# Final state products of three head groups made in the hole of the second norm of a decoder step

## The chip, the core and the metric

The kernel runs on one core of one Trainium2 chip and is written against the engines directly: TensorE (PE, with its weight loads PEld shown apart), VectorE (DVE), ScalarE (ACT), GpSimd (POOL) and SyncE (SP), which issues most DMAs. The metric is the device time of one execution in microseconds, as the median of repeated runs.

## The reference, cut to what matters

The reference is one step of a one-layer hybrid decoder: 256 prompt tokens (two chunks of 128) and 64 sample tokens (8 sequences of 8) with a width of 2048, all in fp32.

```python
h = rms_norm(x, norm_mix_pre); proj = h @ w_in        # gMLP u, v | SSD z, x, B, C, dt
gate_out = gelu(u) * (tril(W_s) @ layer_norm(gelu(v)) + b_s)       # chunks of 128
ssm_out, new_ssm = ssd_mixer(z, xbc, dt, state, ...)               # 32 heads of 64, 4 groups
x = x + rms_norm(concat(gate_out, ssm_out) @ w_out, norm_mix_post) # the second norm
f = (gelu(g) * u) @ ffn_w_down,  g, u = split(conv(rms_norm(x, norm_ffn_pre) @ ffn_w_up))
x = x + rms_norm(f, norm_ffn_post)
```

Inside the SSD mixer the state of a head runs over the two prompt chunks. The state after the last chunk is an output of its own (`ssm_state_prompt`, `o_ssm_p` in the kernel): the state after chunk 0, decayed by the whole of chunk 1, plus the sum over the tokens s of chunk 1 of (decay from s to the end) * dt_s x_s B_s^T. This sum is the "final state product" below. For a group of 8 heads it is one product of a 128x128 matrix (tokens by state) with a 128x512 matrix (tokens by 8 heads of 64), in plain fp32. Nothing else in the step needs it.

## The kernel before, in words

All 320 tokens lie in the free dimension of one tile per 128 features (`NT` = 320, `KD` = 16 tiles for the width of 2048). Every large product is taken as three: weights and activations are split into a high part rounded to fp32r and a low part, the remainder, and `ps` gathers hi x hi, lo x hi and hi x lo (L153, L154, L155; L190 for the first block of the up projection, whose products go through all column blocks with the high part of the weights first). The weights come through SP in slabs of 512 KB (`wraw`, three buffers). For each slab ACT writes the high part (`whi`, L124) and DVE subtracts it for the low part (`wlo`, L125), each in one instruction of 128x1024. `split` (L401, L402) does the same for activations: ACT scales and rounds, DVE makes the remainder.

The stages follow one another on PE: projection and gMLP part; four SSD head groups, whose steps are written as generators (`ssd(g)`) and pulled along by the projections that run around them (`tick`), so that their small products lie scattered between the weight products; `w_out` in eight chunks of features (`chunk_out`), summed into `acc`; the second norm; `ffn_w_up` and `ffn_w_down`; the last norm.

A tile framework orders the instructions of each engine by their place in the program, by priorities (`first()` and `high_priority` pull work ahead), and by `issue_after(x)`, which keeps an instruction behind x. It also puts in the waits between engines. PSUM has two pools of four banks each: `mm` for the weight products and `misc` for the small ones (tags `mm` and `ms`). Each `misc` call takes the next bank and waits until that bank's last reader is done.

At the end of `ssd(g)` the kernel makes `x1d`, the decayed inputs of chunk 1 (L851, POOL, a tile named `xde`), and decays the state of chunk 0 in place (`s1`, L1027, POOL). The generator `final()` then makes the final state product into `fin_ps` (L1032, PE), adds it to `s1` (L1034, DVE) and stores it. Groups 0 to 2 do this inside the group. Group 3's is kept in the list `rest` for the second norm.

The second norm is the one place where PE has no large products ready. Behind the last product of `w_out` come the token sums of squares (`tsum`, L294), group 3's final state product, and the root: DVE scales (L279, L281), ACT takes the square root (L282), DVE refines the inverse root (L283 to L286). PE spreads the result over the partitions with three transposes (`spread`, L302). Meanwhile `idle_products` (L817) has PE make products that nobody reads: one of 128x512 ahead of the spread, seven behind it, all fp32r. Then `x1_ready(k0, nk)` makes the blocks of the normed input one by one, each through DVE scale (L1141), DVE add of the residual (L1142), ACT high part (L401) and DVE low part (L402). The first products of `ffn_w_up` (L190) take each block as soon as it is there. POOL has little to do in that stretch; it makes squares for norms (L335) in others. On SP, behind the last weight slabs of the groups, come `cs` loads (L837, from `dacs_d`), the small loads of the last group's norm (L324), and then the slabs of `w_out`.

Of the kernel before, what the change touches and what calls it, by code (L numbers as in the profile page):

```python
# [9 lines left out]
F32 = mybir.dt.float32  # L10
F32R = mybir.dt.float32r
I32 = mybir.dt.int32
AF = mybir.ActivationFunctionType
ALU = mybir.AluOpType
# [3 lines left out]
P = 128  # L18
# [3 lines left out]
NT = NP + NS  # L22
# [12 lines left out]
def hybrid_step(  # L35
# [10 lines left out]
    act, dve, pool, pe, sp = nc.scalar, nc.vector, nc.gpsimd, nc.tensor, nc.sync  # L46
# [4 lines left out]
    dr = ctx.enter_context(tc.tile_pool(name="dr", bufs=1, space=DRAM))  # L51
# [5 lines left out]
    def misc(name):  # L57
        return ms.tile([P, 512], F32, tag="ms", name=name)
# [6 lines left out]
    with tc.high_priority(offset=300000):  # L65
        dve.memset(ones, 1.0)

        ps = misc("early")
# [31 lines left out]
    def col(i):  # L100
        return prm[:, i:i + 1]
# [166 lines left out]
        rsqrt_ins.append(ins)  # L268
        return r

    rsqrt_ins, sums_ins, spread_ins, rooted, low = [], [], [], [], []

    def rsqrt_by_root(rest, ps, scale, rows=P):

# [14 lines left out]
    def token_sums(*sqs):  # L289

        ps = misc("tsum")
        for c, o in enumerate((0, P, NT - P)):
            for i, sq in enumerate(sqs):
                ins = pe.matmul(ps[:, c:c + 1], sq[:, o:o + P], ones[:, 0:1], start=i == 0, stop=i == len(sqs) - 1).ins  # L294
        sums_ins.append(ins)
        return ps[:, 0:3]
# [40 lines left out]
    def squares_of(total):  # L337

        one, held = [], []

        def step(nb):
            if nb < KD - 3:
                add_square(total, acc[:, nb, :], nb == 0)
                if nb == 0:

                    act.activation(tp.tile([P, 1], F32, name="root_there", bufs=1), total[:, 0:1], AF.Sqrt)
                return
            with first():
                if nb < KD - 1:
                    held.append(misc("sq_ps")[:, :NT])  # L350
                else:
                    one.append(tp.tile([P, NT], F32, tag="sq", name="sq", bufs=2))
                for ts in parts_of(nb):
                    act.activation((one or held)[-1][:, ts], acc[:, nb, ts], AF.Square)
                if nb > KD - 3:
                    dve.tensor_tensor(out=total, in0=total, in1=held.pop(0), op=ALU.add)
        return step, one


    dacs_d = dr.tile([NH, NT + NS], F32, name="dacs_d")  # L360
    tot_d = dr.tile([NH, NB], F32, name="tot_d")
    ssq_d = [dr.tile([P, NT // 32], F32, name=f"ssq_d{i}") for i in range(4)]


# [30 lines left out]
    def split(hi, lo, x, scale=None):  # L395

        if scale is None:
            act.copy(hi, x)
            made = dve.tensor_tensor(out=lo, in0=x, in1=hi.bitcast(F32), op=ALU.subtract)
        else:  # L400
            act.activation(hi, x, AF.Copy, scale=scale)  # L401
            made = dve.scalar_tensor_tensor(out=lo, in0=x, scalar=scale, in1=hi.bitcast(F32), op0=ALU.mult, op1=ALU.subtract)  # L402

        return made.ins
# [16 lines left out]
    with ExitStack() as mctx:  # L421
        op = mctx.enter_context(tc.tile_pool(name="op", bufs=1))
# [153 lines left out]
        with tc.tile_pool(name="gp", bufs=1) as gp:  # L576
# [60 lines left out]
            for n in range(2):  # L637
                ps = banks("ps_v")
                for kt in range(KD):
                    x = [h[:, kt, :] for h in hT], xs_two[kt // 8][:, kt % 8, :]  # L640
                    cs = V0 + 1024 * n
# [38 lines left out]
                with first():  # L680
                    for c, g in ((0, 0), (0, 1), (1, 0), (1, 1), (2, 0), (2, 1)):
                        at, src = slice(0, NS if c == 2 else P), ps[c][g]
                        if c == 2:
# [4 lines left out]
                                                       scale=r[at, c:c + 1]).ins)  # L688
# [99 lines left out]
        with tc.tile_pool(name="sd", bufs=1) as sd:  # L788
# [23 lines left out]
            x_of = {0: x0}  # L812
            rest = []

            def idle_products(ps, n):
                for _ in range(n):
                    ins = pe.matmul(ps, bsp[:, 0, :P], bsp[:, 0, :], start=True, stop=True).ins  # L817
                return ins

            def ssd(g):  # L820

                xs = x_of[g]
# [125 lines left out]
                def end(i, by=act):  # L948
                    made = grown(sts[i], bms.pop(i))
                    store_state(i, sts[i], by)  # L950
                    return made
# [75 lines left out]
                pool.tensor_tensor(out=by_head(s1), in0=by_head(s1),  # L1027
                                   in1=dec[:, 2, h0:h0 + 8].unsqueeze(2).to_broadcast([P, 8, 64]), op=ALU.mult)

                def final():  # L1030
                    ps = misc("fin_ps")
                    made = pe.matmul(ps, btok[:, 1, bs], x1d, start=True, stop=True)  # L1032
                    yield made.ins
                    dve.tensor_tensor(out=s1, in0=s1, in1=ps, op=ALU.add)  # L1034
                    (pool if g == 3 else act).dma_start(o_ssm_p[g], s1)
                    yield
                if g == 3:
                    rest.extend([lambda: end(3, pool), final()])
                else:
                    yield  # L1040
                    yield
                    for _ in final():
                        pass

            tasks = [ssd(g) for g in range(4)]
            res = [[] for _ in range(4)]
# [50 lines left out]
            finish(norm3)  # L1097
            sq2 = hp.tile([P, NT], F32, tag="ssq", name="sq2")

            squares, one = squares_of(sq2)  # L1100
            chunk_out(w_out, 7, *res[3], False, squares, apart=True)

# [4 lines left out]
            with first():  # L1107
                with tc.issue_after(pd_last[-1]), tc.issue_after(added_last[0]):
                    made = rest[0]()
                with tc.issue_after(made):  # L1110
                    most = token_sums(sq2)
                with tc.issue_after(sums_ins[-1]):
                    ps = token_sums(*one)
                with tc.issue_after(sums_ins[-1]):
                    made = next(rest[1])
                r = rsqrt_by_root(most, ps, 1.0 / D)
                behind = rsqrt_ins[-1]

                idle = misc("idle")
                with tc.issue_after(made):  # L1120
                    made = idle_products(idle, 1)
                with tc.issue_after(made):
                    r2b = spread(r)
                with tc.issue_after(spread_ins[-1]):
                    idle_products(idle, 7)
            sq3 = hp.tile([P, NT], F32, tag="ssq", name="sq3")


# [6 lines left out]
            def x1_ready(k0, nk):  # L1135
                for kt in range(k0, k0 + nk):
                    q, k = kt // 4, kt % 4
                    a = acc[:, kt, :]
                    with first() if kt < 2 else tc.high_priority(offset=100000):
                        with tc.issue_after(added[0]) if kt == 1 else nullcontext():  # L1140
                            dve.scalar_tensor_tensor(out=a, in0=a, scalar=col(prm_at["norm"][0] + kt), in1=r2b, op0=ALU.mult, op1=ALU.mult)  # L1141
                        added.append(dve.tensor_tensor(out=a, in0=a, in1=xr[q][:, k, :], op=ALU.add).ins)  # L1142
                        low.append(split(hT[0][:, kt, :], hT[1][:, kt, :], a, col(prm_at["norm"][1] + kt)))
                        if k == 3 and q < 2:
                            load_x(q + 2)
            load_x(0)
            load_x(1)
            up0 = []
            project(ffn_w_up, 0, None, late=up0, ready=x1_ready, after=behind, ahead=1, more=DFF, held=added)
            with tc.issue_after(low[2]):  # L1150
                next(rest[1])

            room = [op.tile([P, 4, NT], F32, tag="xs", name="sq_two", bufs=2) for _ in range(2)]
            total, *some = [t[:, i:i + 2, :] for t in room for i in (0, 2)]
# [7 lines left out]
    x1 = acc  # L1162
# [273 lines left out]
```

## Time and profile before

| what | value |
|---|---|
| time, median of 3 runs | 1775.49 us (1774.15 to 1775.97) |
| the profiled execution's own time | 1774.69 us |
| span in its profile | 1773.0 us |
| PE busy | 1765.1 us, 100% |
| PE weight loads | 1711.9 us, 97% |
| DVE busy | 1173.7 us, 66% |
| ACT busy | 817.9 us, 46% |
| POOL busy | 274.5 us, 15% |
| granted TensorE clock | 0.999 of full |
| moved by DMA | 290.01 MB |

The span runs from the first to the last instruction that the profiler saw; the execution's own time has a little more around it. Busy times are sums over the whole span, so they tell which engine is the bound on average and not in which stage. A row of the timeline reads: start in us, duration in us, engine, source line, operation, written tile <- read tiles, shape, and the number of like instructions that follow one another in it; the brackets give the idle time before it and who ended it. A row of a group reads: smallest / median / largest duration in ns, then the first and the last start.

### The profile page before, as it was taken

The numbers are of one execution on the slowest core, as the hardware profiler recorded it, in microseconds if no ns is written. First come the engines' busy times: TensorE is split into PE (matmuls) and PEld (weight loads), VectorE is DVE, ScalarE is ACT, GpSimd is POOL, SyncE is SP. The second block draws the span as 40 slices with busy tenths as digits, with TensorE's granted clock in tenths as the row PEclk, the third lists the DMA queues.
The fourth block names the chain that finished last, engine by engine and source line by source line (L and its number), as shares of the span: only waits on it lengthen the run. The fifth ranks groups of instructions, "written<-read, shape, count | busy, mean of one in ns | idle before, by whom it ended". The sixth has DMA issues, their size and how long they took to land.

```text
span 1773.0 us, 30633 instructions
## 1 busy us (share of the span) xinstructions
PE 1765.1 (100%) x11897; PEld 1711.9 (97%) x11897; DVE 1173.7 (66%) x2015; ACT 817.9 (46%) x1193; POOL 274.5 (15%) x602
## 2 busy tenths in 40 slices
PE   9999999999999999999999999999999999999998
PEld 7789999999999998999999999999999999999998
DVE  7549764657978778678865465656657575656575
ACT  5434555334564556445645334343434343333445
POOL 1202200000331313103211011010102010101004
PEclk9999999999999999999999999999999999999999
DMA  7556645455666666555554554555455544454542
GB/s 261 161 150 171 189 141 159 153 152 182 223 189 195 186 203 188 147 179 158 171 158 147 154 153 148 155 148 153 150 151 158 144 156 145 156 155 145 155 151 102
DMA packets 217297, 290.01 MB, mean 164 GB/s; under 512 B 19264, under 2 KB 146624, under 8 KB 216960
## 3 DMA queue, kind: packets, MB, share of 16 engines
q1 hardware_dynamic: 205424, 268.84, 50.1%
q10 hardware_dynamic: 10016, 14.16, 2.2%
q0 software_dynamic: 1712, 5.05, 1.0%
q8 instruction: 94, 1.54, 0.4%
q14 instruction: 51, 0.42, 0.1%
HBM read 273.17 MB, written 14.84 MB: 162 GB/s over the span
## 4 chain that ended last, share of the span: by engine, by line
PE 98%; DVE 1%; issue 0%; ACT 0%; ACTq 0%; DVEq 0%
PE ps L153 19%; PE ps L154 19%; PE ps L155 19%; PE pd L153 10%; PE pd L155 10%; PE pd L154 10%; PE ps_v L144 7%; PE y_ps L1004 1%; PE up_ps L925 0%; PE sg L752 0%; PE yo_ps L908 0%; PE xt_ps L414 0%; PE early L70 0%; PE x1p L1299 0%; DVE xsp L863 0%
## 5 line engine op out<-in xcount | busy, mean ns | idle before, releaser
L125 DVE TENSOR_TENSOR wlo<-wraw,whi 128x1024 fp32r<-128x1024 f32 (+1 forms) x476 | 582.3, 1223 | 421.4 <-ACT whi L124 419.6
L124 ACT CAST whi<-wraw 128x1024 fp32r<-128x1024 f32 (+1 forms) x475 | 495.1, 1042 | 714.5 <-PE ps L154 381.5
L153 PE MATMUL ps<-h_hi,whi 128*128 128x320 f32 x2268 | 700.6, 309 | 0.0
L154 PE MATMUL ps<-h_lo,whi 128*128 128x320 f32 x2268 | 699.3, 308 | 0.0
L155 PE MATMUL ps<-h_hi,wlo 128*128 128x320 f32 x2268 | 698.9, 309 | 0.0
L153 PEld LDWEIGHTS ps<-h_hi,whi 128*128 128x128 f32 x2268 | 425.7, 188 | 2.5 <-issue 1.6
L154 PEld LDWEIGHTS ps<-h_lo,whi 128*128 128x128 f32 x2268 | 425.8, 188 | 0.7
L155 PEld LDWEIGHTS ps<-h_hi,wlo 128*128 128x128 f32 x2268 | 425.6, 188 | 0.0
L155 PE MATMUL pd<-fhi,wlo 128*128 128x320 f32 x704 | 217.0, 308 | 0.0
L153 PE MATMUL pd<-fhi,whi 128*128 128x320 f32 x704 | 217.0, 308 | 0.0
L154 PE MATMUL pd<-flo,whi 128*128 128x320 f32 x704 | 217.0, 308 | 0.0
L153 PE MATMUL pd<-ohi,whi 128*128 128x320 f32 x448 | 139.1, 310 | 0.0
L155 PE MATMUL pd<-ohi,wlo 128*128 128x320 f32 x448 | 138.4, 309 | 0.0
L154 PE MATMUL pd<-olo,whi 128*128 128x320 f32 x448 | 138.1, 308 | 0.0
L153 PEld LDWEIGHTS pd<-fhi,whi 128*128 128x128 f32 x704 | 132.2, 188 | 0.0
L154 PEld LDWEIGHTS pd<-flo,whi 128*128 128x128 f32 x704 | 132.2, 188 | 0.0
L155 PEld LDWEIGHTS pd<-fhi,wlo 128*128 128x128 f32 x704 | 132.2, 188 | 0.0
L1201 POOL COPY ptf<-pad 128x2 f32<-128x2 f32 x88 | 21.0, 238 | 602.7 <-DVE pad L1189 601.9
L249 DVE TENSOR_TENSOR acc_ffn<-acc_ffn,pd 128x320 f32<-128x320 f32 (+1 forms) x161 | 77.5, 482 | 37.8 <-PE pd L155 36.3
L153 PEld LDWEIGHTS pd<-ohi,whi 128*128 128x128 f32 x448 | 84.1, 188 | 1.6 <-issue 1.0
L154 PEld LDWEIGHTS pd<-olo,whi 128*128 128x128 f32 x448 | 84.1, 188 | 0.3
L155 PEld LDWEIGHTS pd<-ohi,wlo 128*128 128x128 f32 x448 | 84.1, 188 | 0.2 <-issue 0.2
(335 smaller groups left out, 1866.5 us busy)
## 6 DMA issues: line engine op xcount, KB each, us to landing
wraw<-in_ffn_w_up SPq DMA_DIRECT2D x176, 512.0 KB, 3.6
wraw<-in_w_in SPq DMA_DIRECT2D x140, 512.0 KB, 3.8
wraw<-in_ffn_w_down SPq DMA_DIRECT2D x88, 512.0 KB, 3.3
wraw<-in_w_out SPq DMA_DIRECT2D x64, 512.0 KB, 3.4
st<-in_state_ssm SPq DMA_DIRECT2D x32, 256.0 KB, 4.1
out_ssm_state_sample<-st ACTq DMA_DIRECT2D x30, 256.0 KB, 4.1
cs<-dacs_d SPq DMA_DIRECT2D x16, 320.0 KB, 4.7
xr<-in_xT SPq DMA_DIRECT2D x4, 640.0 KB, 4.0
```

The costliest lines, as they stand in the source:

```text
L124: rounded[:] = [act.copy(hi, raw).ins]
L125: dve.tensor_tensor(out=lo, in0=raw, in1=hi.bitcast(F32), op=ALU.subtract)
L144: made = pe.matmul(out, xi, w[g][wi], start=first and begins, stop=last and ends)
L153: pe.matmul(ps, whi, xhi, start=first, stop=False)
L154: pe.matmul(ps, whi, xlo, start=False, stop=False)
L155: return pe.matmul(ps, wlo, xhi, start=False, stop=last).ins
L249: added_last[:] = [dve.tensor_tensor(out=acc[:, nb, ts], in0=acc[:, nb, ts], in1=ps[:, ts], op=ALU.add).ins]
L1004: pe.matmul(ps[64 * i:64 * i + 64, cols], w(hl), x(hl, m, cpx), tile_position=(0, 64 * i), **flags)
L1201: pool.tensor_copy(ptf[:, k, :], pad[:, 256:258])
```

## The change

Groups 0 to 2 no longer make their final state product. Each stores `s1` and `x1d` to DRAM instead, by POOL's queue. Before the last chunk of `w_out` SP loads them again (`load_ends`): the three `x1` into buffers of the tag `cs`, the three `s1` into one buffer of the tag `xdt`. In the hole of the second norm PE makes group 3's product where it stood, group 0's where the one idle product stood, and those of groups 1 and 2 where the seven stood, behind the spread. The idle products are gone. The other half of the new `final(g)` is no longer a DVE addition from PSUM: ACT copies `fin_ps` over `x1d`, POOL adds the copy to `s1`, and POOL issues the store. ACT's copy for group 3 is placed behind its square root, the copies for groups 0, 1 and 2 behind the high parts of blocks 0, 1 and 2 (`high`); the additions and stores are placed last, in the program behind the projection and under `issue_after(low[-1])`.

```diff
@@ -268,7 +268,7 @@
         rsqrt_ins.append(ins)
         return r

-    rsqrt_ins, sums_ins, spread_ins, rooted, low = [], [], [], [], []
+    rsqrt_ins, sums_ins, spread_ins, rooted, low, high = [], [], [], [], [], []

     def rsqrt_by_root(rest, ps, scale, rows=P):

@@ -359,6 +359,7 @@

     dacs_d = dr.tile([NH, NT + NS], F32, name="dacs_d")
     tot_d = dr.tile([NH, NB], F32, name="tot_d")
+    s1_d, x1_d = ([dr.tile([P, 512], F32, name=f"{n}_d{g}") for g in range(3)] for n in ("s1", "x1"))
     ssq_d = [dr.tile([P, NT // 32], F32, name=f"ssq_d{i}") for i in range(4)]


@@ -398,7 +399,7 @@
             act.copy(hi, x)
             made = dve.tensor_tensor(out=lo, in0=x, in1=hi.bitcast(F32), op=ALU.subtract)
         else:
-            act.activation(hi, x, AF.Copy, scale=scale)
+            high.append(act.activation(hi, x, AF.Copy, scale=scale).ins)
             made = dve.scalar_tensor_tensor(out=lo, in0=x, scalar=scale, in1=hi.bitcast(F32), op0=ALU.mult, op1=ALU.subtract)

         return made.ins
@@ -812,11 +813,6 @@
             x_of = {0: x0}
             rest = []

-            def idle_products(ps, n):
-                for _ in range(n):
-                    ins = pe.matmul(ps, bsp[:, 0, :P], bsp[:, 0, :], start=True, stop=True).ins
-                return ins
-
             def ssd(g):

                 xs = x_of[g]
@@ -1027,20 +1023,34 @@
                 pool.tensor_tensor(out=by_head(s1), in0=by_head(s1),
                                    in1=dec[:, 2, h0:h0 + 8].unsqueeze(2).to_broadcast([P, 8, 64]), op=ALU.mult)

-                def final():
-                    ps = misc("fin_ps")
-                    made = pe.matmul(ps, btok[:, 1, bs], x1d, start=True, stop=True)
-                    yield made.ins
-                    dve.tensor_tensor(out=s1, in0=s1, in1=ps, op=ALU.add)
-                    (pool if g == 3 else act).dma_start(o_ssm_p[g], s1)
-                    yield
                 if g == 3:
-                    rest.extend([lambda: end(3, pool), final()])
+                    at_end[g] = s1, x1d
+                    rest.append(lambda: end(3, pool))
                 else:
+                    pool.dma_start(s1_d[g], s1)
+                    pool.dma_start(x1_d[g], x1d)
                     yield
                     yield
-                    for _ in final():
-                        pass
+
+            at_end = {}
+
+            def load_ends():
+                s1s = sd.tile([P, 3, 512], F32, tag="xdt", name="s1s", bufs=1)
+                for g in range(3):
+                    x1 = sd.tile([P, 2, NT], F32, tag="cs", name="x1s", bufs=3).rearrange("p i n -> p (i n)")[:, :512]
+                    sp.dma_start(x1, x1_d[g])
+                    sp.dma_start(s1s[:, g], s1_d[g])
+                    at_end[g] = s1s[:, g], x1
+
+            def final(g):
+                ps = misc("fin_ps")
+                s1, x1d = at_end[g]
+                yield pe.matmul(ps, btok[:, 1, P * g:P * g + P], x1d, start=True, stop=True).ins
+                act.copy(x1d, ps)
+                yield
+                pool.tensor_tensor(out=s1, in0=s1, in1=x1d, op=ALU.add)
+                pool.dma_start(o_ssm_p[g], s1)
+                yield

@@ -1097,6 +1107,7 @@
             finish(norm3)
             sq2 = hp.tile([P, NT], F32, tag="ssq", name="sq2")

+            load_ends()
             squares, one = squares_of(sq2)
             chunk_out(w_out, 7, *res[3], False, squares, apart=True)

@@ -1111,18 +1122,21 @@
                     most = token_sums(sq2)
                 with tc.issue_after(sums_ins[-1]):
                     ps = token_sums(*one)
+                ends = [final(g) for g in range(4)]
                 with tc.issue_after(sums_ins[-1]):
-                    made = next(rest[1])
+                    made = next(ends[3])
                 r = rsqrt_by_root(most, ps, 1.0 / D)
                 behind = rsqrt_ins[-1]
-
-                idle = misc("idle")
+                with tc.issue_after(rooted[-1]):
+                    next(ends[3])
                 with tc.issue_after(made):
-                    made = idle_products(idle, 1)
+                    made = next(ends[0])
                 with tc.issue_after(made):
                     r2b = spread(r)
-                with tc.issue_after(spread_ins[-1]):
-                    idle_products(idle, 7)
+                made = spread_ins[-1]
+                for g in (1, 2):
+                    with tc.issue_after(made):
+                        made = next(ends[g])
             sq3 = hp.tile([P, NT], F32, tag="ssq", name="sq3")


@@ -1141,14 +1155,18 @@
                             dve.scalar_tensor_tensor(out=a, in0=a, scalar=col(prm_at["norm"][0] + kt), in1=r2b, op0=ALU.mult, op1=ALU.mult)
                         added.append(dve.tensor_tensor(out=a, in0=a, in1=xr[q][:, k, :], op=ALU.add).ins)
                         low.append(split(hT[0][:, kt, :], hT[1][:, kt, :], a, col(prm_at["norm"][1] + kt)))
+                        if kt < 3:
+                            with tc.issue_after(high[-1]):
+                                next(ends[kt])
                         if k == 3 and q < 2:
                             load_x(q + 2)
             load_x(0)
             load_x(1)
             up0 = []
             project(ffn_w_up, 0, None, late=up0, ready=x1_ready, after=behind, ahead=1, more=DFF, held=added)
-            with tc.issue_after(low[2]):
-                next(rest[1])
+            for g in range(4):
+                with tc.issue_after(low[-1]):
+                    next(ends[g])

             room = [op.tile([P, 4, NT], F32, tag="xs", name="sq_two", bufs=2) for _ in range(2)]
             total, *some = [t[:, i:i + 2, :] for t in room for i in (0, 2)]
```

## The prediction

> **What bounds the kernel now.** I read the page first (busy shares and the chain), then TensorE's waits, then the timeline of the hole behind the second norm, then the rows of what is moved.
>
> ```profile
> span 1773.0 us, 30633 instructions
> PE 1765.1 (100%) x11897; PEld 1711.9 (97%) x11897; DVE 1173.7 (66%) x2015; ACT 817.9 (46%) x1193; POOL 274.5 (15%) x602
> ...
> PE 98%; DVE 1%; issue 0%; ACT 0%; ACTq 0%; DVEq 0%
> ...
> PE early L70 <- DVE ones L66: 1.1, 1, 1.1
> ...
> PE spread L302 <- DVE rs_r L286: 0.7, 2, 0.4
> ...
> PE up_ps L925 <- DVE xsp L863: 0.5, 2, 0.2
> ...
> PE ps L190 <- ACT h_hi L401: 0.2, 1, 0.2
> ```
>
> PE is the bound nearly everywhere: 98% of the chain, and its waits for others add up to 2.5 us in 1773. So a PE instruction taken out of the stream is worth its slot, and any other engine costs nothing until it makes PE wait. The profiled execution took 1774.69 us, its span plus 1.69, which is 0.80 below the median of the runs (1775.49). I make the sum against 1774.69 and add 0.80.
>
> The one place where others lead is the hole. PE squares up the norm, waits, and starts the up projection as soon as the first normed block is there:
>
> ```profile
> 821.30 1.10 PE L1032 MATMUL fin_ps<-xde,btok 128*128 128x512 f32 x2
> ...
> 821.84 0.80 PE L817 MATMUL idle<-bsp 128*128 128x512 f32 x1
> ...
> 822.02 1.03 ACT L124 CAST whi<-wraw 128x1024 fp32r<-128x1024 f32 x1
> ...
> 823.06 0.51 PE L302 MATMUL spread<-ident,rs_r 128*128 128x128 f32 x3 [0.42 <-DVE rs_r L286]
> ...
> 823.33 1.85 PE L817 MATMUL idle<-bsp 128*128 128x512 f32 x7
> ...
> 823.61 0.55 DVE L1141 SCALAR_TENSOR_TENSOR acc_mix<-acc_mix,prm,spread 128x320 f32<-128x320 f32 x1 [0.70 <-PE spread L302]
> ...
> 824.19 0.49 DVE L1142 TENSOR_TENSOR acc_mix<-acc_mix,xr 128x320 f32<-128x320 f32 x1
> ...
> 824.72 0.56 ACT L401 ACTIVATE h_hi<-acc_mix,prm 128x320 fp32r<-128x320 f32 x1 [1.67 <-DVE acc_mix L1142]
> ...
> 825.34 0.85 PE L190 MATMUL ps<-h_hi,whi 128*128 128x320 f32 x4 [0.16 <-ACT h_hi L401]
> ...
> 826.84 0.55 DVE L402 SCALAR_TENSOR_TENSOR h_lo<-acc_mix,prm,h_hi 128x320 fp32r<-128x320 f32 x1
> ...
> 827.79 0.31 PE L154 MATMUL ps<-h_lo,whi 128*128 128x320 f32 x1
> ...
> 830.75 1.22 DVE L125 TENSOR_TENSOR wlo<-wraw,whi 128x1024 fp32r<-128x1024 f32 x1
> ...
> 832.92 0.31 PE L155 MATMUL ps<-h_hi,wlo 128*128 128x320 f32 x1
> ```
>
> From spread to L190 the path is DVE scale, DVE add, ACT split. Behind 825.34 PE reads what DVE has only just written: the low part of block 1 is done at 826.84 + 0.55 = 827.39 and read at 827.79 (slack 0.40); the low half of the third slab is done at 830.75 + 1.22 = 831.97 and read some 0.9 later (51 products of 0.147 behind 825.34, about 832.9).
>
> **The change, part by part.** *Three products leave the stream.* What one costs there:
>
> ```profile
> 502.93 0.31 PE L155 MATMUL ps<-h_hi,wlo 128*128 128x320 f32 x1
> ...
> 503.08 1.02 PE L1032 MATMUL fin_ps<-xde,btok 128*128 128x512 f32 x2
> ...
> 503.93 1.04 PE L414 MATMUL xt_ps<-ident,xs 128*128 128x128 f32 x8
> ...
> L1032 PE MATMUL fin_ps<-xde,btok x8: 590/592/676, 503.1 to 821.8; 128*128 128x512 f32 x8
> ```
>
> Each product is two passes, and the next instruction starts 503.93 - 503.08 = 0.85 us behind it. Three of them: -2.55 us, at places where PE is dense. By durations, which overlap, it would be 6 x 0.592 = 3.55; I take the slots, since start to start is what PE loses, and keep 3.55 as the far end. The three DVE additions (0.69 each) and the three ACT stores that go with them were under PE: 0.
>
> *Three products enter the hole.* One stands in place of the single idle product. The array is then taken from about 822.25 to 823.10, so the transposes start 0.05 late. Two (1.70 us) stand where seven idle ones were (1.85): they end near 825.1, before L190. Cost 0.05. If that cover were gone, each would cost its 0.85.
>
> *Four ACT copies.* The nearest row is the copy of the first state product, 0.58:
>
> ```profile
> L899 ACT COPY s<-s_ps x4: 578/580/580, 441.6 to 691.4; 128x512 f32<-128x512 f32 x4
> ...
> L984 POOL TENSOR_TENSOR cpx<-cpx,cT x16: 724/737/1510, 440.2 to 726.3; 128x256 f32<-128x256 f32 x16
> ...
> L335 POOL TENSOR_TENSOR sq<-sq,sq x24: 877/889/1860, 798.1 to 1752.0; 128x320 f32<-128x320 f32 x24
> ...
> L851 POOL TENSOR_TENSOR xde<-xdt,dec x8: 1041/1044/1489, 439.0 to 695.8; 128x512 f32<-128x512 f32 x8
> ```
>
> The first, of group 3, waits for its product (822.40) and runs until about 823.06; the weight cast queued behind it moves from 822.02 to 823.06 and ends at 824.1, before ACT is wanted at 824.72. The others follow the splits of blocks 0, 1 and 3; ACT is idle there between splits (h_hi of block 1 does not start before 826.04). Cost 0; without that gap, 0.58 each.
>
> *Four POOL additions, and this is where it is decided.* The source puts them behind the last low split, but that is an instruction of DVE and the additions run on POOL; in the changed instruction order they wait for nothing but their own copies and loads. So they start at about 823.2, 826.3, 828.7 and 831, in the middle of DVE's ramp. No such addition is in the trace. Two full operands take 0.737 at 256 elements and 0.889 at 320, 2.4 ns an element, so 1.34 at 512; the lower end is 1.04, the 512-wide row whose second operand repeats. I take 1.3, since both operands are full. What POOL and DVE do to each other:
>
> ```profile
> 813.68 1.23 DVE L125 TENSOR_TENSOR wlo<-wraw,whi 128x1024 fp32r<-128x1024 f32 x1 [0.45 <-ACT whi L124]
> ...
> 814.16 1.48 POOL L335 TENSOR_TENSOR sq<-sq,sq 128x320 f32<-128x320 f32 x1 [0.79 <-ACT sq L334]
> ...
> 449.90 1.76 DVE L993 TENSOR_TENSOR cs<-cs,cb_cms 128x320 f32<-128x320 f32 x2
> ...
> 450.19 2.40 POOL L919 TENSOR_TENSOR st<-st,tote 128x512 f32<-128x512 f32 x2 [0.61 <-PE yo_ps L908]
> ...
> 499.91 2.02 POOL L1027 TENSOR_TENSOR s<-s,dec 128x512 f32<-128x512 f32 x1
> ...
> 500.95 0.54 DVE L1014 SCALAR_TENSOR_TENSOR xs<-xs,prm,y_ps 128x320 f32<-128x320 f32 x1
> ```
>
> The POOL addition of 814.16 takes 1.48 instead of 0.89: it stood still until DVE's L125 (two SBUF inputs) let go near 814.8. At 449.90 two DVE instructions take 1.76 instead of 0.89: the second waited out one POOL instruction that got in between, so the two alternate. L1014, whose second input is in PSUM, keeps its 0.54 under a POOL instruction. So an addition stops L1142, L402 and L125 (two SBUF inputs), and not L1141 (0.46 from start to start), which reads the spread from PSUM. [...]
>
> Addition of group 3: 823.2 to 824.5; L1142 of block 0 wants to start at 824.24, so about 0.3 late, straight onto L190. [...] DVE is late by 0.3 + 3 x 0.85 = 2.85 at the third slab's low half, up to 0.3 + 3 x 1.3 = 4.2 if nothing runs beside. The 0.9 of slack there goes off: PE loses 1.95 to 3.3, and I take 2.5, nearer to the first because POOL and DVE take turns. With additions of 1.04 the same sum gives 0.05 + 3 x 0.58 - 0.9 = 0.9. [...]
>
> *Stores and reloads.* Six stores on POOL and six loads on SP, 256 KB each. POOL is busy 15%. On SP one load goes behind the last cs load, the rest behind the small loads:
>
> ```profile
> 721.89 0.37 SPq L837 DMA_DIRECT2D cs<-dacs_d  x1
> ...
> 724.11 15.38 SPq L118 DMA_DIRECT2D wraw<-in_w_in  x5
> ...
> 743.12 1.86 SPq L324 DMA_DIRECT2D small<-ssq_d  x4
> ...
> 746.62 8.99 SPq L118 DMA_DIRECT2D wraw<-in_w_out  x3
> ```
>
> SP has 2 us free before 724.11 and 1.6 before 746.62, and the weight loads behind come one in 3 to 4.5 us; an issue is 0.37. The load that needs group 3's buffers waits for its last product, at 745.4, still ahead of 746.62. The data is there 70 us before it is used. Cost 0; if a weight load came late it would cost PE up to a landing, about 4 us.
>
> Sum: -2.55 + 0.05 + 2.5 = 0.0 on 1774.69, so 1774.7 for a like execution and 1775.5 for the median.
>
> **Rivals.** [...] (3) The reloads hold up weight loads on SP: one landing, +4, 1779.5; against it the free 1.6 us above. That the products do not move is excluded by the instruction order: three are gone from the groups and three stand in the hole.
>
> **How the numbers follow.** 0.2% is 3.55 us, about what a measurement of this kernel tells from no change. Forecast 0.42; (1) 0.28; (2) 0.22; (3) 0.08. Half of (1) passes 3.55 if slots are worth their durations and the runs' own spread (1774.15 to 1775.97) adds: faster 0.14. Of (2) 0.18 and of (3) 0.06 pass it: slower 0.24. Same: 0.62. The forecast's own range is 1773.9 (additions of 1.04) to 1776.3. The range 1771.5 to 1780.5 leaves out some 0.06 below and 0.12 above.
>
> **What would show it.** Right: fin_ps three times between 821 and 825 (less 2.5), none near 503, 595 and 684; PE up to the hole about 2.5 us earlier; in the ramp new PE waits for DVE h_lo and wlo, 2 to 3 us together; L402 and L1142 stretched to 1.5 us where POOL adds. Wrong: DVE's rows keep 0.49 and 0.55 beside POOL's additions (then it is faster), additions above 2 us, or PE waiting before the hole.

## The result

| | median us | lowest to highest | runs |
|---|---|---|---|
| before | 1774.95 | 1773.47 to 1776.52 | 20 |
| changed | 1779.39 | 1775.39 to 1787.45 | 20 |

The ratio is 1.0030, with a 95% interval of 1.0021 to 1.0039: slower by about 0.3%. (This ratio and those below are taken over all the runs of both kernels and are not the ratios of the medians, which are 4.44 us apart here.) That is more than the 0.2%, 3.55 us, that the prediction took as the least that such a measurement tells. The runs of the changed kernel also spread four times as wide. The forecast was 1775.5 with a range of 1771.5 to 1780.5. The median lies in the range, but on the slower side, which had a chance of 0.24.

The profiled execution took 1777.14 us. From its page, and from TensorE's waits (us in total, times, longest):

```profile
span 1775.4 us, 30653 instructions
PE 1764.6 (99%) x11889; PEld 1710.1 (96%) x11889; DVE 1175.7 (66%) x2011; ACT 818.6 (46%) x1197; POOL 283.0 (16%) x615
...
PE 97%; DVE 1%; DMA 0%; issue 0%; ACT 0%; POOL 0%; POOLq 0%; ACTq 0%
...
PE up_ps L921 <- DVE xsp L859: 2.6, 2, 2.4
...
PE ps L154 <- DVE h_lo L403: 0.9, 1, 0.9
PE ps L190 <- DVE h_lo L403: 0.6, 1, 0.6
```

PE does 0.5 us less work than before and the span is 2.4 us longer. New are 1.5 us of waits for low parts in the ramp (`h_lo`), which the prediction counted, and a wait of 2.4 us for `xsp` inside a head group, which it did not. (`xsp` holds the inputs of the sample tokens, whose low part DVE makes by a subtraction; `up_ps` is the state product that reads it.)

I matched the instructions of PE in the two traces one by one and took the difference of their starts. It shows where the time comes and goes (span against span; 0.7 us are there from the first microseconds on, a matter of the single execution):

| place, time in before | after minus before, us |
|---|---|
| first weight products, 20 | +0.70 |
| ahead of group 0's product, 502 | +1.49 |
| behind it, 504 | +0.63 |
| behind group 1's, 595 | -0.09 |
| behind group 2's, 685 | -0.93 |
| group 3's start, 700 to 820 | +1.18 |
| first products of `ffn_w_up`, 825.34 | +1.22 |
| end of the ramp, 840 | +3.67 |
| last products of `ffn_w_down`, 1755 | +3.77 |

Each product that left gave 0.85 or 0.86. One group start took 2.13 back (-0.95 to +1.18 at 699), the ramp took 2.45, and 0.6 went at 496, where a `cs` load landed late; e3 below, which is the kernel before up to this place, has a wait there too. The last norm, which the change leaves alone, gave 1.4 back. About 1.0 of it is the clock: the profiled execution of before ran at half its clock there for 3.41 us, from 1759.45 to 1762.86, the changed kernel's did not, and the difference of starts falls from +4.06 to +3.08 in that stretch.

The hole and the ramp behind it, in the timeline of the changed kernel:

```profile
822.49 1.10 PE L1048 MATMUL fin_ps<-xde,btok 128*128 128x512 f32 x2
...
823.43 1.02 PE L1048 MATMUL fin_ps<-x1s,btok 128*128 128x512 f32 x2
...
824.30 1.27 POOL L1051 TENSOR_TENSOR s<-s,xde 128x512 f32<-128x512 f32 x1 [0.74 <-ACT xde L1049]
...
824.62 1.88 PE L1048 MATMUL fin_ps<-x1s,btok 128*128 128x512 f32 x4
...
825.40 0.52 DVE L1156 TENSOR_TENSOR acc_mix<-acc_mix,xr 128x320 f32<-128x320 f32 x1
...
826.56 0.87 PE L190 MATMUL ps<-h_hi,whi 128*128 128x320 f32 x4
...
827.08 1.31 POOL L1051 TENSOR_TENSOR s1s<-s1s,x1s 128x512 f32<-128x512 f32 x1 [0.65 <-ACT x1s L1049]
...
827.16 1.57 DVE L403 SCALAR_TENSOR_TENSOR h_lo<-acc_mix,prm,h_hi 128x320 fp32r<-128x320 f32 x1
...
828.78 0.85 PE L190 MATMUL ps<-h_lo,whi 128*128 128x320 f32 x4 [0.61 <-DVE h_lo L403]
829.11 1.80 DVE L403 SCALAR_TENSOR_TENSOR h_lo<-acc_mix,prm,h_hi 128x320 fp32r<-128x320 f32 x1
829.26 1.30 POOL L1051 TENSOR_TENSOR s1s<-s1s,x1s 128x512 f32<-128x512 f32 x1
...
830.97 0.42 PE L154 MATMUL ps<-h_lo,whi 128*128 128x320 f32 x1 [0.89 <-DVE h_lo L403]
```

The hole itself cost nothing: four products stand in it, the spread comes as it did, and the first product of `ffn_w_up` has the same distance to the state product ahead of it as before (826.56 - 822.49 = 4.07 against 825.34 - 821.30 = 4.04). The additions begin in the ramp and take 1.27 to 1.33. The low part of block 0 (L403, 827.16) starts 0.08 behind an addition and takes 1.57 in place of 0.55. The next one, of block 1, takes 1.80 although it is recorded 0.15 ahead of its addition (829.11 and 829.26). PE waits behind both.

Now the start of group 3, first before and then after:

```profile
696.45 1.44 DVE L125 TENSOR_TENSOR wlo<-wraw,whi 128x1024 fp32r<-128x1024 f32 x1
...
696.77 3.51 POOL L919 TENSOR_TENSOR st<-st,tote 128x512 f32<-128x512 f32 x2
...
698.52 0.84 DVE L863 TENSOR_TENSOR xsp<-xq,xsp 64x512 fp32r<-64x512 f32 x1
...
699.51 0.47 PE L925 MATMUL up_ps<-xsp,bm 128*128 128x512 f32 x1 [0.25 <-DVE xsp L863]
```

```profile
695.81 2.33 POOL L915 TENSOR_TENSOR st<-st,tote 128x512 f32<-128x512 f32 x2
...
697.12 2.10 DVE L125 TENSOR_TENSOR wlo<-wraw,whi 128x1024 fp32r<-128x1024 f32 x1
...
699.85 0.69 DVE L859 TENSOR_TENSOR xsp<-xq,xsp 64x512 fp32r<-64x512 f32 x1
...
700.69 0.47 PE L921 MATMUL up_ps<-xsp,bm 128*128 128x512 f32 x1 [2.37 <-DVE xsp L859]
```

Before, the low half of a weight slab (L125) starts 0.32 ahead of POOL's two state shrinks (`st`), and the subtraction of `xsp` slips in between them. After, POOL is there first: L125 starts when the first shrink is done and the second has begun, takes 2.10, `xsp` comes 1.33 later, and PE, which was 0.95 early, waits 2.37.

Where DVE begins to be late is seen some 12 us earlier, at the group's start (after):

```profile
683.56 0.58 POOL L1030 DMA_DIRECT2D s_d<-s  x1 [0.30 <-POOL s L1023]
...
684.17 0.74 POOL L980 TENSOR_TENSOR cpx<-cpx,cT 128x256 f32<-128x256 f32 x1
...
684.66 2.34 DVE L125 TENSOR_TENSOR wlo<-wraw,whi 128x1024 fp32r<-128x1024 f32 x1 [0.15 <-ACT whi L124]
684.86 1.05 POOL L847 TENSOR_TENSOR xde<-xdt,dec 128x512 f32<-128x512 f32 x1
```

The issue of the new store of `s1` (L1030) stands ahead of a POOL product (`cpx`, L980), which before ran from 683.72 to 684.46. Now it runs until 684.91. L125 starts while it runs, POOL's decay product `xde` follows it at once, and L125 takes 2.34 in place of 1.22.

### The profile page after: what moved, and what is told of

The parts are those of the page before. It is cut to its first block, busy times and chain, and to the rows that moved or that the text cites. A ratio compares the mean times of both kernels' runs of the same rounds, so it can differ in the third digit from the quotient of the medians.

```text
span 1775.4 us, 30653 instructions
## 1 busy us (share of the span) xinstructions
PE 1764.6 (99%) x11889; PEld 1710.1 (96%) x11889; DVE 1175.7 (66%) x2011; ACT 818.6 (46%) x1197; POOL 283.0 (16%) x615
## 4 chain that ended last, share of the span: by engine, by line
PE 97%; DVE 1%; DMA 0%; issue 0%; ACT 0%; POOL 0%; POOLq 0%; ACTq 0%
PE ps L153 19%; PE ps L155 19%; PE ps L154 19%; PE pd L153 10%; PE pd L155 10%; PE pd L154 10%; PE ps_v L144 7%; PE y_ps L1000 1%; PE up_ps L921 1%; PE sg L753 0%; PE yo_ps L904 0%; PE xt_ps L415 0%; DMA cs<-dacs_d 0%; PE early L70 0%; PE x1p L1317 0%
## 5 line engine op out<-in xcount | busy, mean ns | idle before, releaser
L125 DVE TENSOR_TENSOR wlo<-wraw,whi 128x1024 fp32r<-128x1024 f32 (+1 forms) x476 | 585.4, 1230 | 423.0 <-ACT whi L124 421.1
```

What stands on the lines that cost most here:

```text
L125: dve.tensor_tensor(out=lo, in0=raw, in1=hi.bitcast(F32), op=ALU.subtract)
```

## The experiments

All times are medians; "before" was run beside each experiment (1774.95 to 1775.36). Theory: the additions in the ramp are the loss. Rivals: the head groups themselves (the start of a group without its product), or the stores and reloads.

**e1, additions really last, on POOL.**

```diff
+            gate = op.tile([P, 1], F32, name="gate")
+            with tc.issue_after(low[-1]):
+                gated = pool.tensor_copy(gate, hT[1][:, KD - 1, 0:1].bitcast(F32)).ins
             for g in range(4):
-                with tc.issue_after(low[-1]):
+                with tc.issue_after(gated):
                     next(ends[g])
```

> The changed kernel with one instruction more: POOL copies one column of the last block's low part ahead of its four additions, so that the additions and their stores really come last. Theory A (the additions in the ramp lock DVE out; PE's stalls there are what costs 2.5 us, and what makes the granted clock drop in some executions): the stalls of PE behind 826 are gone, the profiled execution falls from 1777.1 to about 1774.6, every run has a clock of 0.999 or 1.000 and the runs lie within 3 us. Theory B (the spread of the runs comes from the hole itself, whose idle products are gone, or from the head groups): 2.5 us of stall go too, but runs still reach 1785 at clocks of 0.996 to 0.998.

Measured: 1779.13 (1774.97 to 1782.16, 12 runs), ratio 1.0017 (1.0007 to 1.0028). The ramp is clean: PE is as far behind at 840 as at 820 (5.12 in the matching of starts). But the additions now meet the weights' low halves:

```profile
860.51 3.52 POOL L1051 TENSOR_TENSOR s1s<-s1s,x1s 128x512 f32<-128x512 f32 x2
860.52 2.35 DVE L125 TENSOR_TENSOR wlo<-wraw,whi 128x1024 fp32r<-128x1024 f32 x1
```

```profile
PE up_ps L921 <- DVE xsp L859: 5.3, 3, 2.7
...
PE ps_one L155 <- DVE wlo L125: 0.9, 1, 0.9
```

That costs 1.3 by 880, half of what the ramp had cost. And the profile has 5.3 us of `up_ps` waits, nearly all in groups 2 and 3, and the runs still spread over 7 us. So theory A held for the ramp and fell for the spread, and the median is only 0.3 below that of the changed kernel.

**e2, the four additions on DVE** (`dve.tensor_tensor` in `final`, where the order behind the last low part holds).

> The changed kernel with the four additions on DVE in place of POOL; there the order behind the last low part holds. Theory A: like e1, 1774.6 with no spread; DVE has room for four additions of 0.69 us by then. Theory B: the spread stays as in the changed kernel. Rival for both: the additions now hold up DVE's low parts of weights, and PE loses up to 2.8 us behind the ramp in place of 2.5 in it, 1777.

Measured: 1775.74 (1773.90 to 1780.69, 11 runs), ratio 1.0000 (0.9991 to 1.0009). No wait for `h_lo` is left; the longest that is left is a head group's:

```profile
PE up_ps L921 <- DVE xsp L859: 2.6, 2, 2.4
```

Against the changed kernel this is 3.65 us; the same exchange in e6 and e5 below gives 2.54, and in e16 and e15 1.49. The mean of the three is 2.6. The matched starts are steadier: the ramp adds 2.4 to 2.5 in all three profiles with the additions on POOL in it (the changed kernel, e6, e16), and in e2 nothing (+0.71 from 702 on, +0.74 at 880). The rest of the spread is there.

**e3, the products only left out**: the kernel before without the product and the addition in groups 0 to 2.

```diff
-                    for _ in final():
-                        pass
+                    act.dma_start(o_ssm_p[g], s1)
```

> The kernel before without the three products, their copies and additions in groups 0 to 2 (the states of three groups are stored without their last term); the hole is as before, idle products included. Theory A: PE gains its slots, 3 x 0.85, so 1774.95 - 2.55 = 1772.4. Rival: leaving the products out shifts the start of the next group so that POOL and DVE collide there, and 2.1 us come back before 700: 1774.5.

Measured: 1774.73 (1773.62 to 1777.60, 11 runs), ratio 0.9994 (0.9986 to 1.0003). Only 0.55 of the 2.55 us show (1775.28 beside it), and that is not clear of noise. The rival is right, although at group 2 and not at group 3, where the matched starts give 2.4 back between 596 and 612:

```profile
597.12 1.04 POOL L851 TENSOR_TENSOR xde<-xdt,dec 128x512 f32<-128x512 f32 x1 [4.28 <-DVE xdt L845]
...
597.31 1.93 DVE L125 TENSOR_TENSOR wlo<-wraw,whi 128x1024 fp32r<-128x1024 f32 x1 [0.28 <-ACT whi L124]
...
608.10 2.53 POOL L919 TENSOR_TENSOR st<-st,tote 128x512 f32<-128x512 f32 x2 [0.57 <-PE yo_ps L908]
608.15 1.55 DVE L863 TENSOR_TENSOR xsp<-xq,xsp 64x512 fp32r<-64x512 f32 x1
...
609.76 0.50 PE L925 MATMUL up_ps<-xsp,bm 128*128 128x512 f32 x1 [1.32 <-DVE xsp L863]
```

**e4, e3 with the stores and reloads** (on the queues of the changed kernel).

> e3 with the six stores on POOL's queue and the six reloads on SP's (nothing reads the reloaded x1; the states are stored from the reloaded copy, again without their last term). If the DMAs cost nothing: as e3, within 0.5 us. If they delay the loads of the next group and of weights: 0.6 to 2.7 us over e3, with PE waits between 490 and 700 that e3 does not have.

Measured: 1777.05 (1772.70 to 1781.87, 12 runs), ratio 1.0008 (0.9996 to 1.0019). Its best runs are the best of all kernels, its worst 9 us above. The transfers cost 2.3 us over e3 in the median, and 2.8 from e7 to e8 below, the same step. The profiled execution of e4 took 1773.61, near its lowest; it has no wait at group 2 and one of 2.38 at group 3, as that of the changed kernel has.

**e5 to e8, a wait at a group's start.** In e3 the decay product `xde` on POOL starts 0.2 ahead of L125, which then takes 1.93 (597.12 and 597.31 above). The edit copies one column of the second half of `xdt` on POOL, with the product placed behind it in the source, in e2 (e5), the changed kernel (e6), e3 (e7) and e4 (e8). Theory C: two such starts side by side, at groups 2 and 3, are the spread and half of the loss, and the product and its addition on DVE had kept them apart. With the wait e6 would then take 1775.0 and e5 1772.4, with runs within 3 us.

```diff
-                    if c == 0:
-                        x0d = decayed(0, 0)
+                gate = sd.tile([P, 1], F32, tag="gate", name="gate", bufs=1)
+                pool.tensor_copy(gate, xdt[:, 1, 0:1])
+                x0d = decayed(0, 0)
```

> The changed kernel with one POOL instruction more per group: the first decay product of a group (xde) waits, by a copy of one column, for the second half of xdt, so that it no longer starts at the same moment as the weights' low half on DVE. [...] Theory D (the stores and reloads make the spread, by the queues or memory): runs still reach 1782.

> e2 (additions on DVE) with the same wait at the start of a group. Theory C: no up_ps wait, no ramp stall: 1774.95 - 2.55 = 1772.4, runs within 3 us; it would beat both kernels. Theory D: 1775 to 1776 with runs up to 1780.

> e3 (no products, additions, stores or reloads for groups 0 to 2; their states are stored without the last term) with the same wait. Theory C: the whole 2.55 us show: 1772.4, against 1774.7 for e3. If the stalls of e3 have another cause: 1774.7 again.

> e4 (e3 with stores and reloads) with the same wait. Theory C: as e7, 1772.4 to 1772.9, runs within 3 us: the DMAs themselves cost nothing. Theory D: 1777 with runs up to 1782, as e4.

Measured: e6 1782.23 (8 runs, ratio 1.0033), e5 1779.69 (11, 1.0019), e7 1774.57 (11, 0.9996), e8 1777.41 (12, 1.0010). They do not test what they were meant to: nothing ties the product to the copy, and it was issued ahead of it, at the old place. In all four profiles POOL then comes first at group 2, by 0.20 or 0.21; whether the copy did that is not shown. What follows from it is told by the profile of e5:

```profile
595.63 1.04 POOL L847 TENSOR_TENSOR xde<-xdt,dec 128x512 f32<-128x512 f32 x1 [4.31 <-DVE xdt L841]
...
595.84 1.92 DVE L125 TENSOR_TENSOR wlo<-wraw,whi 128x1024 fp32r<-128x1024 f32 x1 [0.28 <-ACT whi L124]
...
606.35 0.59 POOL L1032 DMA_DIRECT2D x_d<-xde  x1 [0.30 <-POOL xde L847]
...
606.67 2.92 DVE L859 TENSOR_TENSOR xsp<-xq,xsp 64x512 fp32r<-64x512 f32 x1
...
606.96 2.08 POOL L916 TENSOR_TENSOR st<-st,tote 128x512 f32<-128x512 f32 x2
...
609.65 0.71 PE L922 MATMUL up_ps<-xsp,bm 128*128 128x512 f32 x1 [2.70 <-DVE xsp L859]
```

POOL starts 0.21 ahead of L125 and DVE is late from then on. Some 10 us later the issue of the `x1` store (L1032, 0.59) stands between the second decay product and the two shrinks, pushes them onto `xsp`, which takes 2.92, and PE waits 2.70.

Put side by side, the eleven profiles of the variants in which `xde` is not held back give a table without exception for group 2:

| who starts first near 596 | store of `x1` ahead of the shrinks | profiles | longest `up_ps` wait in group 2 |
|---|---|---|---|
| L125, by 0.05 to 0.17 | yes | after, e2, e4 | none |
| POOL, by 0.19 to 0.21 | no | e3, e7, e15, e16 | 1.32 or 1.33 |
| POOL, by 0.07 to 0.21 | yes | e1, e5, e6, e8 | 2.69 to 2.71 |

(In the changed kernel's own profile L125 starts at 596.68 and takes 1.22, `xde` at 596.85 and takes 1.96. In e3 and e5 `xde`, first there, takes 1.04 and L125 1.93 and 1.92. The one that starts second takes longer; why it does is not shown. Before, apart from each other, they took 1.04 and 1.22.) The changed kernel, e1 and e2 have the same instructions in the groups, and the order came out both ways, so it is a matter of the execution; with one profile of each, how often is not shown. The recorded start alone does not always tell which of two instructions will take longer, though: L403 at 829.11 above is 0.15 ahead of POOL's addition and yet takes 1.80, `xsp` in e5 is 0.29 ahead of the shrinks and yet takes 2.92, and at group 3 L125 is up to 0.44 ahead of `xde` and yet takes 2.14 to 2.58, behind a `cpx` that is still running, in all nine of these profiles that have the stores. e3 and e7, without stores, have no such wait at group 3. That fits what the group's start showed above, but no run moved the store of `s1` away from `cpx`.

Before, `xde` started 1.90 behind L125 at group 2, and the question did not arise:

```profile
595.80 0.69 DVE L1034 TENSOR_TENSOR s<-s,fin_ps 128x512 f32<-128x512 f32 x1 [0.44 <-PE fin_ps L1032]
...
596.41 1.22 DVE L125 TENSOR_TENSOR wlo<-wraw,whi 128x1024 fp32r<-128x1024 f32 x1
...
598.31 1.04 POOL L851 TENSOR_TENSOR xde<-xdt,dec 128x512 f32<-128x512 f32 x1 [6.70 <-DVE xdt L845]
```

DVE had the addition of the state product (L1034) ahead of L125 and the multiplication that makes `xdt` (L845, from 597.54) behind it, and `xde` waits for `xdt`. Without the addition the multiplication goes ahead of L125.

**e9 and e11, the wait made real** (the copy writes into the product's own tile) in e2 and in e4.

```diff
-                def decayed(i, c):
+                def decayed(i, c, after=None):
                     xde = sd.tile([P, 512], F32, tag="xde", name="xde", bufs=2)
+                    if after is not None:
+                        pool.tensor_copy(xde[:, 0:1], after)
...
-                    if c == 0:
-                        x0d = decayed(0, 0)
+                x0d = decayed(0, 0, after=xdt[:, 1, 0:1])
```

Theory C's time is 1772.4 for both, with runs within 3 us.

> e2 (additions on DVE), and now the first decay product of a group really waits for the second half of xdt (the one-column copy writes into its own tile, so that the order on POOL holds; in e5 to e8 the copy was made, but the product was put ahead of it). [...] Theory D (the stores and reloads themselves): the start moves, but the runs still spread from 1774 to 1780.

> e4 (no products and additions for groups 0 to 2, stores and reloads kept, the hole as before; three states are stored without their last term) with the same real wait. Theory C: 1772.4 within 0.5, runs within 3 us, against 1777.05 for e4. Theory D: 1777 with runs up to 1782 as e4 and e8.

Measured: e9 1782.88 (1780.51 to 1784.18, 5 runs), e11 1782.31 (1780.77 to 1785.76, 5 runs). Ratios 1.0038 and 1.0039. The product does start 2.1 to 2.2 behind L125 in groups 2 and 3, and group 3's wait is gone (0.26 and 0.25, as before). But the later product pushes the `x1` store and the shrinks onto `xsp` elsewhere, in group 2 again (waits of 2.78 and 3.17) and now in group 0 too:

```profile
450.85 0.59 POOL L1032 DMA_DIRECT2D x_d<-xde  x1
...
451.35 2.75 DVE L861 TENSOR_TENSOR xsp<-xq,xsp 64x512 fp32r<-64x512 f32 x1
...
454.15 0.79 PE L922 MATMUL up_ps<-xsp,bm 128*128 128x512 f32 x1 [3.06 <-DVE xsp L861]
```

So theory C, that this one race is the spread, falls as it was put: taking it away made the time worse, as long as the store sits where it does. Theory D's times (1777 for e11) were missed as well.

**e16 and e15, the stores at the end of the group** (as the source has them), in the changed kernel and in e2; `shrunk_s1` is the decay of `s1` (L1023).

```diff
-                    pool.dma_start(s1_d[g], s1)
-                    pool.dma_start(x1_d[g], x1d)
+                    with tc.issue_after(shrunk_s1):
+                        pool.dma_start(s1_d[g], s1)
+                        pool.dma_start(x1_d[g], x1d)
```

> The changed kernel with one thing different: POOL issues each store of x1 only behind the decay of s1, at the end of the group, as the source has it; in the changed kernel it goes out as soon as x1 is made, in the middle of a group's start, between the decay product and the two state shrinks (st). Theory E (the issue of 0.58 us, and the wait ahead of it, push the two shrinks together onto DVE's subtraction of xsp, which then takes 2.92 instead of 0.7 to 1.5 us, PE waits 2.7 us at up_ps, and the granted clock falls for a while): no xsp above 1.6 us at 600 to 615, the clock stays at 0.999 or above, runs within 4 us, and what is left is -2.55, a wait of up to 2.1 at the start of group 3, and the ramp's 2.5: 1775 to 1777, against 1779.4. Theory D (the amount that is stored and reloaded): 1779 again.

> The same with the four additions on DVE (as e2). Theory E: 2.5 us below the kernel above, 1772.5 to 1774.5, and the best of all that keep the whole result; theory D: as e2, 1775.7 with runs up to 1780.

Measured: e16 1778.23 (1775.76 to 1783.58, 11 runs), ratio 1.0019 (1.0009 to 1.0029); e15 1776.74 (1774.17 to 1778.37, 11 runs), ratio 1.0004 (0.9995 to 1.0013). At group 2 theory E holds (e15's profile):

```profile
607.48 2.53 POOL L915 TENSOR_TENSOR st<-st,tote 128x512 f32<-128x512 f32 x2 [0.56 <-PE yo_ps L904]
607.54 1.55 DVE L859 TENSOR_TENSOR xsp<-xq,xsp 64x512 fp32r<-64x512 f32 x1
...
609.14 0.50 PE L921 MATMUL up_ps<-xsp,bm 128*128 128x512 f32 x1 [1.32 <-DVE xsp L859]
```

In this profile too `xde` starts 0.20 ahead of L125, and still `xsp` takes 1.55 and PE waits 1.32, as in e3. The times that theory E gave did not come. They were 1775 to 1777 for e16 and 1772.5 to 1774.5 for e15, with a clock of 0.999 or above and runs within 4 us; e16 spreads over 7.8 and both have runs at 0.998. The highest runs come down by 4 (e16, of 11 runs, against the changed kernel, of 20) and 2 (e15 against e2). The medians say less: e16 is 1.2 below the changed kernel, e15 1.0 above e2, inside their spreads. Group 3's wait of 2.4 stays, where the stores still stand ahead of `cpx`, and e16's profile has a wait of 2.29 at 579 that no other has. No kernel that keeps the whole result came out below before; the best, e2, equals it.

**The clock.** The last part of the spread is the granted clock. One-microsecond windows of e5, PE alone (us, PE busy, clock, DMA share, GB/s):

```profile
609.00:610.00 1.00, 0.35 (x1) 0.89 0.00 0
610.00:611.00 1.00, 1.00 (x5) 0.50 0.00 0
...
612.00:613.00 1.00, 1.00 (x5) 0.50 0.90 332
613.00:614.00 1.00, 1.00 (x8) 0.91 0.51 193
```

Behind the wait of 2.70 PE runs at half its clock for 3.4 us and loses 1.7 more. In the 14 profiles there are 18 PE waits of 2.29 to 3.17 us in the groups; 12 had such a stretch (nine of 3.4 us, three of 6.8) beginning within 1.2 us of their end, 6 had not, and no shorter wait in the groups or the ramp had. The same wait of 2.4 at group 3 fell to half clock in e1, e5, e6 and e16, where the matched starts lose 3.6 or 3.7 in all, and not in the changed kernel, e2, e4, e8 and e15, where they lose 2.1. The last norm is a place of its own: three profiles (before, e1, e15) have a stretch of 3.41 there, and PE has no wait above 0.5 ahead of it. So the kernel before has such stretches too. What decides whether a wait is followed by one is not shown. In the 20 runs of the changed kernel the mean clock goes from 1.000 (1775.39 to 1778.93) down to 0.996 (1787.45), and 10 of them are at 0.998 or below; in e3 1 of 11 is, in e7 none.

## Why the prediction was right and wrong

The time lies in the range that was given, but that is luck: the upper part of the range was there for additions of 2.1 us, rival (2), and for a weight load that comes late, rival (3), and neither is what happened. The additions took 1.3 us and not 2.1, and PE waited for no weight load. The three terms of the forecast's sum held. But a sign of being wrong that it named came ("PE waiting before the hole", 2.37 at 699), and PE reached the hole 1.2 us later than before and not 2.5 earlier.

*Three products leave: right in the term.* 0.85 each was forecast; the matched starts show 0.86, 0.85 and 0.86.

*Three products enter, ACT copies: right.* 0.05 was forecast; the distance from the state product to L190 grew by 0.03.

*The additions in the ramp: right in what they do to DVE and in the sum, not in the path.* That they do not wait for the last low part, 1.3 us each (measured 1.27 to 1.33), DVE's instructions longer by up to one addition, 2.5 us for PE: the matched starts give 2.45, and three exchanges of POOL for DVE give 1.49, 2.54 and 3.65. It shows in the rows that were named, in the low parts (L402, now L403, at 1.57 and 1.80) and in PE's waits for `h_lo`; but the loss falls on blocks 0 and 1, in waits of 0.61 and 0.89, and not at the third slab's low half, and the first addition cost nothing: the residual addition of block 0 (L1156 at 825.40, 0.58 behind its scale as before) kept 0.52 beside it, where 0.3 had been put down. The last addition cost PE next to nothing either. No run shows the 0.85 that the sum takes for each of three additions; in its place the trace has the low parts 1.02 and 1.25 longer beside the second and third, and beside the fourth (832.93) a scale that keeps its 0.53 (L1155 at 833.03) and a residual addition of 1.13 (L1156 at 833.49, 0.49 before). So two additions did what the sum laid on four with a slack of 0.9 taken off, and that 2.45 is so near to 2.5 is in part luck. Rival (1), additions that cost PE nothing, falls by these 2.45.

*The additions and stores that leave the groups "were under PE: 0": this is the step that failed.* The addition L1034 cost PE nothing itself, but it kept DVE's L125 ahead of `xdt`, and so POOL's `xde` 1.9 us behind L125. Without it the two start within 0.2 us of each other at group 2, and the first to come decides. e3, which has nothing else of the change, keeps 0.55 of 2.55 in its median, and e7, which adds only the copies that held nothing, 0.38.

*Stores on POOL ("POOL is busy 15%", "Cost 0"): failed with it.* What counted was not how busy POOL is, but that the issue of 0.58 stands ahead of POOL's shrinks and pushes them onto DVE's `xsp`, which took 2.92 in e5 in place of 0.69. From e3 to e4 the median rises by 2.3. In group 2, where POOL starts first, the wait is 1.32 without the store of `x1` in between and 2.70 with it. The wait of group 3, the longest in the changed kernel's profile, is in all nine profiles with stores in which `xde` is not held back; there the store of `s1` stands ahead of `cpx`. The reloads on SP and the weight loads, the third rival, showed no wait of PE.

*The clock* has no term in the prediction. It is what turns a loss of 2.1 at group 3 into one of 3.6, in some executions. An estimate of its share: the mean clock is 0.9986 over the 20 runs of the changed kernel and 0.9993 to 0.9995 over those of before beside the experiments, and the difference of 0.0007 to 0.0009 is 1.2 to 1.6 us of 1775.

Sum for the profiled execution, on span: +0.70 at the start, +0.79 ahead of and in group 0's end (0.6 of it at 496), -2.57 for the products, +0.13 between them, +2.13 at group 3, +0.04 in the hole, +2.45 in the ramp, +0.1 behind it, -1.4 in the last norm: 2.4. The terms at the start, around 496 and in the last norm are not the change's own and come to 0.1 together. The forecast had the products and the ramp, and these two cancelled as forecast; what it had not is group 3. The fastest of the 20 runs, at full clock (1775.39 to 1775.84), are where the forecast was; but the profile shows that a group's wait can be in a run at full clock, so the agreement of those runs is not proof that they have none.

Left open: which part of the spread is the group starts and which is the stores alone, since the two interact (the table above). That the store of `s1` makes the wait of group 3 is read from the traces; the wait is absent in e3 and e7 (no stores) and in e9 and e11 (`xde` held back), but in e3 and e7 `cpx` also runs later, behind a `cs` load, and no run changed the store's place alone. The kernel that would join the wait of e9 with the late stores of e15 was not run.

## What to carry to other kernels

A small operation on an engine that is not the bound can still be what keeps two others apart. Before a step is taken out, look at what starts behind it on its engine, and whether something on an engine beside which its instructions take longer (here POOL, beside which L125 took 1.93 in place of 1.22) will then start within a few tenths of a microsecond of it. A store put on a queue that is mostly idle has a place in that queue (its issue took 0.58 here): look at which operation it pushes back, and onto what. A difference in the spread of the runs is a reading of its own: look for the race first, and for its share in the granted clock.

## What was not expected of the hardware

- Two instructions that start 0.05 to 0.21 us apart on DVE and POOL were followed by a wait of PE more than 10 us later or not, by their order: L125 1.22 or 1.92 to 2.05, `up_ps` no wait or 1.32 to 2.71 (group 2, eleven profiles).
- Around a PE pause of 2.29 to 3.17 us came in 12 of 18 cases 3.4 or 6.8 us at half the clock, with pauses up to 1.33 in the groups and the ramp never. In the last norm three of 14 profiles had 3.41 us of it with no pause above 0.5 ahead.
- A subtraction of 64x512 on DVE (0.69 alone) took 2.92 when two POOL operations of 1.06 stood one behind the other: it did not get in between them, while in the trace of before it did (0.84).
